# Experts two pair-buckets at a time, members read from the logits' values alone, and the gather's copies issued behind the router's splits

## The chip, the core and the metric

The kernel runs on one core of one Trainium2 chip. The metric is the device time of one execution in microseconds (us). Engines are named as in the profile: PE is the matrix engine (PEld its weight loads), DVE the vector engine, ACT the scalar engine, POOL GpSimd, SP the engine whose queue issues the DMAs.

## What is computed

Two transformer blocks follow each other on 256 tokens of width 1024, all in float32. The first has four SwiGLU feed-forward layers of width 2816, a gated convolution and a differential attention. The second has a sparse attention, a state-space branch, and at its end a mixture of 32 experts, the only part that the change touches:

```
def hier_moe(h, w_rg, b_rg, w_re, b_re, w_gate, w_up, w_down):     # h: [256, 1024], normed
    g_logits = h @ w_rg + b_rg                     # 4 groups
    g_idx = argmax(g_logits); g_w = softmax(g_logits)[g_idx]
    e_logits = (h @ w_re + b_re).reshape(-1, 4, 8) # 8 experts in a group
    e_in = e_logits[g_idx]
    top_v, top_i = top_k(e_in, 2); top_p = softmax(top_v)
    combine = one_hot(g_idx) * (g_w * sum(one_hot(top_i) * top_p))
    for g in range(4):
        act = silu(h @ w_gate[g]) * (h @ w_up[g]) * combine[:, g]
        out = out + act @ w_down[g]                # w_gate, w_up: 8 x [1024, 256]; w_down: 8 x [256, 1024]
```

Each token uses two experts of one group. The weights of all 32 experts, 100.7 MB, are read in any case.

## The kernel before

The tokens lie in two halves of 128 (`i` = 0, 1). Float32 products of weights and activations in the early layers are made of three products of rounded parts (`hi`, `lo`); `split` (L406) makes such a pair with a copy on ACT (L408) and a subtraction on DVE (L409).

**The way into the experts.** `boundary` (L512) ends the layer before (the output projection `wo`, class `OutProj`) and starts the mixture. For each half it adds `wo` to the residual `h` (L1411), takes the mean square on ACT (L430), the root on POOL (L423), the scaled copy `xs` on DVE (L462, `Moe.pre`), transposes it on PE (L470, `Moe.tr`) and splits it into `xTmoh`, `xTmol` (L408, L409). `Moe.chunk` (L1471) then makes the router's logits `rt` with 16 matmuls, one on `xTmoh` and one on `xTmol` in turn (L1478, L1479), and beside them a second split of `xs`, token by row, into `xh[i]` (ACT, L1481) and `xl[i]` (DVE, L1482), which the gather reads later. In what order the instructions stand on an engine is decided by the framework: a list scheduler with a model of the engines takes, on each engine, a ready instruction, first those of higher priority (`hot`), then the earlier in the program. The engines then run their queues in that order. `issue_after` forbids an order.

**The router.** `route` (L1512) works on DVE with small operations. It takes each token's best group, its two best experts with ties broken by the index (`first_max`), the membership `member` of each token in 16 buckets (a bucket is a pair of neighbouring experts), the token's place in its bucket with five small matmuls (L1540 to L1544), and the selection matrix `S[i]` (128 tokens x 16 buckets x 64 slots, L1551). It also works out the weights of the shares (`cwt`).

**The gather.** `gather` (L1587) multiplies `xh`, `xl` with `S` and so brings the tokens of four buckets at a time into `xg` (32 matmuls for four buckets, 4 calls). `shares` (L1601) does the same for the weights.

**The experts.** The loop over 32 experts (`n`) runs `up(n)`, `down_(n-1)`, `turn_(n)`. `up` (L1609) computes gate and up with 16 products (two instructions each) of 64 stationary columns, gate and up in the two halves of the array's columns; ACT takes silu (L1620), DVE multiplies (L1621). `turn_` transposes 64 rows (L1628). `down_` multiplies with `w_down` (L1640). After each second expert the bucket's sum is split (`yg`), `sgt` transposes `S` (four float32 products, L1653), and `scatter` adds the bucket's rows to `h` with eight matmuls over 64 rows (L1665) and four additions on DVE (L1667). The last one also writes the output.

**The weights' ring.** `Ring` (L1415) loads the expert weights in tiles of 512 KB (4 for gate and up, 2 for down of each expert), 192 tiles in all, from SP's queue (L1430). It has 26 places. A place is loaded anew when PE has read the tile in it.

Of the kernel before, what the change touches and what calls it, by code (L numbers as in the profile page):

```python
# [16 lines left out]
P = 128  # L17
T = 256
# [204 lines left out]
def kernel(ctx: ExitStack, tc: tile.TileContext, a: dict, out: bass.AP, upto=99, start=1):  # L223
# [95 lines left out]
    for n in range(33):  # L319
        if n < 32:  # L320
            for w in ("w_gate_2", "w_up_2"):
                v = a[w][0, n // 8, n % 8].rearrange("(p k) c -> p k c", k=KT)
                ring_src += [v[:, k:k + 4] for k in (0, 4)]
        if n > 0:
            d = a["w_down_2"][0, (n - 1) // 8, (n - 1) % 8]
            ring_src += [d[k * P:(k + 1) * P, :] for k in range(2)]
# [1118 lines left out]
    class Moe(Phase):  # L1445
# [4 lines left out]
        def pre(self, i):  # L1450
            if i == 0:
                self.xs = {}
# [4 lines left out]
                self.lg = self.m1.tile([P, 2, 36], F32, name="lg")  # L1457
# [4 lines left out]
                dve.tensor_scalar(self.iotam, cst[:, C_IOTA:C_IOTA + SLOTS], -1000.0, None, op0=ALU.add)  # L1462
                self.xh = [self.m1.tile([P, KT, P], F32R, name=f"xh{i}") for i in range(2)]
# [7 lines left out]
        def chunk(self, i):  # L1471

            x = xT["mo"]
            c = slice(i * P, (i + 1) * P)
            w = W.get(pl["rt"])
            rt = bank("rt")
            for k in range(KT):
                pe.matmul(rt[:, :72], lhsT=x[0][:, k, c], rhs=w[:, k], start=(k == 0), stop=False)  # L1478
                pe.matmul(rt[:, :36], lhsT=x[1][:, k, c], rhs=w[:, k, :36], start=False, stop=(k == KT - 1))  # L1479
            xv = self.xs[i][:, :].rearrange("t (p k) -> t k p", k=KT)  # L1480
            act.activation(self.xh[i], xv, AF.Copy)  # L1481
            dve.tensor_tensor(out=self.xl[i], in0=xv, in1=self.xh[i].bitcast(F32), op=ALU.subtract)  # L1482
            with hot():
                dve.tensor_tensor(out=self.lg[:, i], in0=rt[:, :36], in1=bc[:, B_RT:B_RT + 36], op=ALU.add)
                dve.tensor_tensor(out=self.lg[:, i], in0=rt[:, 36:72], in1=self.lg[:, i], op=ALU.add)
# [26 lines left out]
        def route(self):  # L1512

            tl, b3, first_max = self.tl, self.b3, self.first_max
            tt, red, lg = dve.tensor_tensor, dve.tensor_reduce, self.lg
            el = lg[:, :, 4:36].rearrange("p i (g e) -> p i g e", e=8)
            gl = lg[:, :, 0:4]
# [14 lines left out]
            oo, m4 = tl("oo", 2, 8), tl("m4", 2, 4)  # L1532
            tt(out=oo, in0=o1, in1=o2, op=ALU.add)
            red(m4, oo[:, :, :].rearrange("p i (b s) -> p i b s", s=2), axis=AX, op=ALU.max)
            M = self.m1.tile([P, 2, 16], BF16, name="member")
            for i in range(2):
                tt(out=M[:, i].rearrange("p (g b) -> p g b", b=4), in0=oh[:, i, :, None].to_broadcast([P, 4, 4]),
                   in1=m4[:, i, None, :].to_broadcast([P, 4, 4]), op=ALU.mult)
            rk = bank("rank")
            pe.matmul(rk[:, 0:16], lhsT=self.before, rhs=M[:, 0], start=True, stop=True)  # L1540
            pe.matmul(rk[:, 16:32], lhsT=self.before, rhs=M[:, 1], start=True, stop=False)
            pe.matmul(rk[:, 16:32], lhsT=self.ones, rhs=M[:, 0], start=False, stop=True)
            pe.matmul(rk[:, 32:48], lhsT=self.ones, rhs=M[:, 0], start=True, stop=False)
            pe.matmul(rk[:, 32:48], lhsT=self.ones, rhs=M[:, 1], start=False, stop=True)  # L1544
            self.rank, place = tl("rank", 3, 16), tl("place", 2, 16)
            dve.scalar_tensor_tensor(place, M, -1000.0, rk[:, :32].rearrange("p (i b) -> p i b", b=16), op0=ALU.mult, op1=ALU.add)
            S = self.S = [self.m1.tile([P, 16, SLOTS], F32R, name=f"S{i}") for i in range(2)]

            def put(b0, b1):
                for i in range(2):  # L1550
                    tt(out=S[i][:, b0:b1], in0=self.iotam[:, None, :].to_broadcast([P, b1 - b0, SLOTS]),  # L1551
                       in1=place[:, i, b0:b1, None].to_broadcast([P, b1 - b0, SLOTS]), op=ALU.is_equal)

            put(0, 4)

# [18 lines left out]
            put(4, 16)  # L1574
            dve.tensor_copy(self.rank[:, :, :].rearrange("p i b -> p (i b)"), rk[:, :48])

        def body(self, _):
            m2, tl, tt = self.m2, self.tl, dve.tensor_tensor
            xh, xl = self.xh, self.xl
            with hot():  # L1580
                self.route()
            S = self.S
            xg = [xtp.tile([P, KT, T], F32, name=f"xg{p}0", tag=f"xT{p}") for p in "hl"]
            cwg = tl("cwg", 32)
            acc, hid, hT, yg, sgT = {}, {}, {}, {}, {}

            def gather(q, ks):  # L1587

                for k in ks:
                    b = bank("xg")  # L1590
                    for kk in range(2):
                        for n, (s, i) in enumerate(((xh, 0), (xh, 1), (xl, 0), (xl, 1))):
                            pe.matmul(b[:, kk * T:(kk + 1) * T], lhsT=s[i][:, k + kk], rhs=S[i][:, 4 * q:4 * q + 4].rearrange("p b s -> p (b s)"),
                                      start=(n == 0), stop=(n == 3))
                    d, s = xg[q][:, k:k + 2], b[:, :].rearrange("p (k t) -> p k t", t=T)
                    if k % 4:
                        act.activation(d, s, AF.Copy)
                    else:
                        dve.tensor_copy(d, s)

            def shares(q):  # L1601
                b = bank("cw")
                for j in range(4):
                    for i in range(2):
                        pe.matmul(b[64:, 2 * j:2 * j + 2], lhsT=S[i][:, 4 * q + j].bitcast(F32), rhs=self.cwt[:, i, 8 * q + 2 * j:8 * q + 2 * j + 2],
                                  start=(i == 0), stop=(i == 1))
                dve.tensor_copy(cwg[64:, 8 * q:8 * q + 8], b[64:, :8])

            def up(n):  # L1609
                ring[0] = 0  # L1610
                b = bank("eg")
                ring[0] = 1
                w = [t[:, :].rearrange("p (k c) -> p k c", c=256) for t in ring_w.get(4)]
                x = xg[n // 8][:, :, n // 2 % 4 * SLOTS:(n // 2 % 4 + 1) * SLOTS]
                for k in range(KT):
                    for v in range(2):
                        pe.matmul(b[64 * v:64 * v + 64, :T], lhsT=x[:, k], rhs=w[2 * v + k // 4][:, k % 4], start=(k == 0), stop=(k == KT - 1))  # L1617
                ring_w.done(4)
                s = m2.tile([P, T], F32, name="es", tag="es")
                act.activation(s[64:], b[:64, :T], AF.Silu)  # L1620
                dve.scalar_tensor_tensor(s[64:], s[64:], cwg[64:, n:n + 1], b[64:, :T], op0=ALU.mult, op1=ALU.mult)  # L1621
                hid[n] = s

            def turn_(n):
                b = bank("eT")
                s = hid.pop(n)
                for k in range(2):
                    pe.transpose(b[:, k * SLOTS:(k + 1) * SLOTS], s[64:, k * P:(k + 1) * P], ident[64:, 64:])  # L1628
                t = m2.tile([P, 2, SLOTS], F32, name="hT", tag="hT")
                act.activation(t, b[:, :2 * SLOTS].rearrange("p (k t) -> p k t", t=SLOTS), AF.Copy)  # L1630
                hT[n] = t

            def down_(n):
                p, e = divmod(n, 2)
                if e == 0:
                    acc[p] = accp.tile([P, 512], F32, name=f"ey{p}", tag=f"acc0{p % 2}")
                t = hT.pop(n)
                for k, w in enumerate(ring_w.get(2)):
                    for j in range(2):
                        pe.matmul(acc[p][64 * j:64 * j + 64], lhsT=t[:, k], rhs=w[:, j * 512:(j + 1) * 512],  # L1640
                                  start=(e == 0 and k == 0), stop=(e == 1 and k == 1))
                ring_w.done(2)
                if e == 1:
                    y = two.tile([P, 2, 512], F32R, name="yg", tag="t")
                    split(acc.pop(p), y[:, 0], y[:, 1])
                    yg[p] = y

            def sgt(p):

                b = bank("SgT")  # L1650
                for i in range(2):
                    for j in range(2):
                        pe.matmul(b[64 * j:64 * j + 64, i * P:(i + 1) * P], lhsT=S[i][:, p].bitcast(F32), rhs=ident, start=True, stop=True)  # L1653
                t = m2.tile([P, T], F32R, name="SgT", tag="SgT")
                act.activation(t, b[:, :T], AF.Copy)
                sgT[p] = t

            def scatter(p):
                y, t = yg.pop(p), sgT.pop(p)
                for i in range(2):  # L1660
# [285 lines left out]
```

## Time and profile before

| | |
|---|---|
| median of 3 runs | 1680.09 us (1673.47 to 1680.95) |
| the profiled execution | 1676.58 us, of which the traced span is 1674.8 us |
| PE busy in the span | 1612.4 us (96%) |
| DVE, ACT, POOL busy | 939.2 us (56%), 786.6 us (47%), 139.7 us (8%) |
| read from HBM in the span | 338.22 MB |
| stretch of the experts (first `up` to the last addition) | 1415.7 to 1668.0 us |

Times in the rows are counted from the start of the span. A busy time of PE is no proof that PE is at its peak, since matmuls overlap; where an engine's work stands on the chain that ended last, its own part is read from that chain.

### The profile page before, as it was taken

What the parts mean: (1) busy time and instruction counts of PE and PEld (TensorE: products, weight loads), DVE (VectorE), ACT (ScalarE), POOL (GpSimd) and SP (SyncE); (2) the same over time, 40 slices, a digit from 0 to 9 for tenths busy, and PEclk for the clock granted to TensorE, in tenths of its full rate; (3) what the DMA queues carried; (4) which work ended last, traced back from release to release, by engine and by line L of the source; (5) the groups of instructions that cost most, each with busy time, mean ns of one, the idle gap of its engine ahead of it and who ended that gap; (6) DMA issues with size and microseconds to landing.
All of it is one profiled execution on the core that took longest, in us unless ns stands there. A gap on an engine that the chain in (4) does not pass through costs nothing.

```text
span 1674.8 us, 28506 instructions
## 1 busy us (share of the span) xinstructions
PE 1612.4 (96%) x11550; PEld 1390.4 (83%) x11550; DVE 939.2 (56%) x1429; ACT 786.6 (47%) x1226; POOL 139.7 (8%) x145
## 2 busy tenths in 40 slices
PE   7999999999999999998999999999999997999997
PEld 7999899999989999986899988988989885555543
DVE  5655666755556555476655556977675655232322
ACT  5544454544445444366544445665767633111111
POOL 1000100000010000024200014400221000000000
PEclk9999999999999999999999999999999997999998
DMA  8766474766647666462566645525443854999991
GB/s 286 253 192 188 151 226 127 235 207 188 198 143 226 193 187 199 152 201 76 161 201 193 191 134 152 151 72 176 121 136 103 297 172 190 407 397 388 414 410 57
DMA packets 211656, 341.21 MB, mean 204 GB/s; under 512 B 14612, under 2 KB 166445, under 8 KB 211389
## 3 DMA queue, kind: packets, MB, share of 16 engines
q1 hardware_dynamic: 211485, 339.24, 61.2%
q8 instruction: 93, 1.52, 0.4%
q14 instruction: 46, 0.38, 0.1%
q0 software_dynamic: 32, 0.07, 0.1%
HBM read 338.22 MB, written 1.05 MB: 203 GB/s over the span
## 4 chain that ended last, share of the span: by engine, by line
PE 81%; DVE 8%; ACT 4%; issue 3%; DMA 2%; POOL 1%; SPq 0%; ACTq 0%; POOLq 0%; DVEq 0%
PE eg L1617 7%; PE g L498 4%; PE u L499 4%; PE u L498 4%; PE g L497 4%; PE g L499 4%; PE u L497 4%; PE fo L400 4%; PE fo L398 4%; PE fo L399 4%; PE ey L1640 3%; DVE lo L176 2%; PE sc L1665 2%; PE tk L400 2%; PE tk L399 2%
## 5 line engine op out<-in xcount | busy, mean ns | idle before, releaser
L176 DVE TENSOR_TENSOR lo<-raw,hi 128x1024 fp32r<-128x1024 f32 (+1 forms) x446 | 523.4, 1184 | 372.2 <-ACT hi L171 365.8
L171 ACT ACTIVATE hi<-raw 128x1024 fp32r<-128x1024 f32 (+1 forms) x434 | 456.4, 1058 | 430.4 <-PE g L498 106.4
L497 PE MATMUL u<-xTh_f,hi 128*128 128x256 f32 x608 | 168.3, 277 | 0.0
L498 PE MATMUL g<-xTl_f,hi 128*128 128x256 f32 x608 | 168.1, 276 | 0.2 <-DVE xTl_f L409 0.2
L497 PE MATMUL g<-xTh_f,hi 128*128 128x256 f32 x608 | 168.2, 277 | 0.1
L498 PE MATMUL u<-xTl_f,hi 128*128 128x256 f32 x608 | 168.0, 276 | 0.0
L499 PE MATMUL u<-xTh_f,lo 128*128 128x256 f32 x608 | 168.0, 276 | 0.0
L499 PE MATMUL g<-xTh_f,lo 128*128 128x256 f32 x608 | 167.9, 276 | 0.0
L398 PE MATMUL fo<-hi,hTh 128*128 128x512 f32 x352 | 138.9, 395 | 0.0
L399 PE MATMUL fo<-lo,hTh 128*128 128x512 f32 x352 | 138.2, 393 | 0.0
L400 PE MATMUL fo<-hi,hTl 128*128 128x512 f32 x352 | 137.8, 393 | 0.0
L498 PEld LDWEIGHTS g<-xTl_f,hi 128*128 128x128 f32 x608 | 114.1, 188 | 1.7 <-DVE xTl_f L409 0.4
L497 PEld LDWEIGHTS g<-xTh_f,hi 128*128 128x128 f32 x608 | 114.2, 188 | 1.6 <-DVE xTl_f L409 0.3
L497 PEld LDWEIGHTS u<-xTh_f,hi 128*128 128x128 f32 x608 | 114.2, 188 | 0.1
L499 PEld LDWEIGHTS u<-xTh_f,lo 128*128 128x128 f32 x608 | 114.2, 188 | 0.0
L498 PEld LDWEIGHTS u<-xTl_f,hi 128*128 128x128 f32 x608 | 114.1, 188 | 0.0
L499 PEld LDWEIGHTS g<-xTh_f,lo 128*128 128x128 f32 x608 | 114.1, 188 | 0.0
L423 POOL TENSOR_TENSOR rstd<-var,mhalf 128x1 f32<-128x1 f32 (+1 forms) x41 | 28.0, 683 | 946.4 <-DVE var L421 894.9
L400 PE MATMUL tk<-hi,xTl_at 128*128 128x256 f32 x320 | 90.6, 283 | 0.0
L399 PE MATMUL tk<-lo,xTh_at 128*128 128x256 f32 x320 | 90.5, 283 | 0.0
L398 PE MATMUL tk<-hi,xTh_at 128*128 128x256 f32 x320 | 90.1, 282 | 0.0
L400 PEld LDWEIGHTS fo<-hi,hTl 128*128 128x128 f32 x352 | 66.2, 188 | 15.2
(475 smaller groups left out, 3531.4 us busy)
## 6 DMA issues: line engine op xcount, KB each, us to landing
raw<-in_ffn_w_gu_dram SPq DMA_DIRECT2D x176, 512.0 KB, 4.4
raw<-in_ffn_w_down_dram SPq DMA_DIRECT2D x88, 512.0 KB, 4.3
raw<-in_w_in_dram SPq DMA_DIRECT2D x72, 512.0 KB, 4.0
mw<-in_w_gate_dram SPq DMA_DIRECT2D x64, 512.0 KB, 7.8
mw<-in_w_up_dram SPq DMA_DIRECT2D x64, 512.0 KB, 7.6
mw<-in_w_down_dram SPq DMA_DIRECT2D x64, 512.0 KB, 8.2
raw<-in_conv_w_in_dram SPq DMA_DIRECT2D x24, 512.0 KB, 4.7
raw<-in_w_kv_dram SPq DMA_DIRECT2D x16, 512.0 KB, 5.3
```

The source lines that it names most:

```text
L171: self.order(self.nc.scalar.activation(hi[:q, :n], r[:q, :n], AF.Copy))
L176: self.order(e.tensor_tensor(out=lo[:q, c:c + cut], in0=r[:q, c:c + cut], in1=hi[:q, c:c + cut].bitcast(F32), op=ALU.subtract))
L398: ms = (pe.matmul(ps, lhsT=xh, rhs=wh, start=first, stop=False), pe.matmul(ps, lhsT=xh, rhs=wl, start=False, stop=False), pe.matmul(ps, lh ...
L399: pe.matmul(ps, lhsT=xh, rhs=wl, start=False, stop=False),
L400: pe.matmul(ps, lhsT=xl, rhs=wh, start=False, stop=last))
L423: pool.tensor_tensor(out=r, in0=v, in1=mhalf[:, :n], op=ALU.pow)
L497: pe.matmul(o, lhsT=wh, rhs=x[0][:, k], start=(k == 0), stop=False)
L498: pe.matmul(o, lhsT=wh, rhs=x[1][:, k], start=False, stop=False)
L499: pe.matmul(o, lhsT=wl, rhs=x[0][:, k], start=False, stop=(k == KT - 1))
L1617: pe.matmul(b[64 * v:64 * v + 64, :T], lhsT=x[:, k], rhs=w[2 * v + k // 4][:, k % 4], start=(k == 0), stop=(k == KT - 1))
L1640: pe.matmul(acc[p][64 * j:64 * j + 64], lhsT=t[:, k], rhs=w[:, j * 512:(j + 1) * 512], start=(e == 0 and k == 0), stop=(e == 1 and k == 1))
L1665: pe.matmul(bs[j], lhsT=t[r, i * P:(i + 1) * P], rhs=y[r, q], start=(q == 0), stop=(q == 1))
```

## The change

**Order of the experts.** `steps` pairs expert `e` of bucket 2m with expert `e` of bucket 2m+1: 16 steps of two experts. The ring's order follows. `up` is now a generator that works on one expert of the step at a time and yields between them; the two experts of a step put their result into the upper and the lower 64 rows of one tile.

**Full height.** `turn_` transposes 128 rows at once, `shares` and `sgt` work on two buckets (128 slots) at once, `sgt` with rounded operands (F32R) and an identity `identr`. `scatter` sums over 128 rows, two buckets at a time, and runs half `i` of the tokens after each half of an `up`. `down_` keeps its size, now with four weight tiles at a time and two banks for the sums.

**Members from values.** The logits are put into 2 x 5 rows of 8 (the four groups' logits, filled up with a very low number, are one row). One maximum, one comparison, one second maximum and one comparison over all rows give the members. The weights of the shares are worked out in `weigh`, behind the first gather.

**Copies behind the splits.** `xh[i]` and `xl[0]` must be issued behind what stands on their engine so far, which is the split `xTmoh`, `xTmol` of that half. `xl[1]` is made in four pieces between the pieces of the first gather. The router's matmuls are ordered: first eight on `xTmoh`, then eight on `xTmol`.

```diff
+    steps = [(4 * m + e, 4 * m + 2 + e) for m in range(8) for e in range(2)]
+    for n in range(17):
+        for x in steps[n] if n < 16 else ():
             for w in ("w_gate_2", "w_up_2"):
...
         if n > 0:
+            ring_src += [a["w_down_2"][0, x // 8, x % 8, k * P:(k + 1) * P, :] for x in steps[n - 1] for k in range(2)]
...
             for k in range(KT):
                 pe.matmul(rt[:, :72], lhsT=x[0][:, k, c], rhs=w[:, k], start=(k == 0), stop=False)
+            for k in range(KT):
                 pe.matmul(rt[:, :36], lhsT=x[1][:, k, c], rhs=w[:, k, :36], start=False, stop=(k == KT - 1))
-            act.activation(self.xh[i], xv, AF.Copy)
-            dve.tensor_tensor(out=self.xl[i], in0=xv, in1=self.xh[i].bitcast(F32), op=ALU.subtract)
+            last = {}
+            for x in nc.cur_bb.bb.instructions:
+                last[x.engine] = x
...
+            r = act.activation(self.xh[i], self.xv[i], AF.Copy).ins
+            issue_after(tc, r, last[r.engine])
+            if i == 0:
+                r = dve.tensor_tensor(out=self.xl[i], in0=self.xv[i], in1=self.xh[i].bitcast(F32), op=ALU.subtract).ins
+                issue_after(tc, r, last[r.engine])
             with hot():
+                dve.tensor_tensor(out=self.part[:, i], in0=rt[:, 36:72], in1=bc[:, B_RT:B_RT + 36], op=ALU.add)
+                dve.tensor_tensor(out=self.lg[:, i, 4:40], in0=rt[:, :36], in1=self.part[:, i], op=ALU.add)
...
+            red(top, lg, axis=AX, op=ALU.max)
+            tt(out=eq, in0=lg, in1=top[:, :, None].to_broadcast([P, 10, 8]), op=ALU.is_equal)
+            dve.scalar_tensor_tensor(low, eq, NEG, lg, op0=ALU.mult, op1=ALU.add)
+            red(t2, low, axis=AX, op=ALU.max)
+            tt(out=low, in0=lg, in1=t2[:, :, None].to_broadcast([P, 10, 8]), op=ALU.is_ge)
+            m4 = tl("m4", 2, 5, 4)
+            red(m4[:, :, :, :].rearrange("p i r b -> p (i r b)"), low[:, :, :].rearrange("p r (b s) -> p (r b) s", s=2), axis=AX, op=ALU.max)
+            for i in range(2):
+                tt(out=M[:, i].rearrange("p (g b) -> p g b", b=4), in0=eq[:, 5 * i, 4:8, None].to_broadcast([P, 4, 4]),
+                   in1=m4[:, i, 1:5], op=ALU.mult)
...
             def shares(q):
+                for j in range(2):
                     for i in range(2):
+                        pe.matmul(b[:, 4 * j:4 * j + 4], lhsT=self.S[i][:, 4 * q + 2 * j:4 * q + 2 * j + 2].rearrange("p b s -> p (b s)").bitcast(F32),
+                                  rhs=self.cwt[:, i, 8 * q + 4 * j:8 * q + 4 * j + 4], start=(i == 0), stop=(i == 1))
...
             def turn_(n):
                 for k in range(2):
-                    pe.transpose(b[:, k * SLOTS:(k + 1) * SLOTS], s[64:, k * P:(k + 1) * P], ident[64:, 64:])
+                    pe.transpose(b[:, k * P:(k + 1) * P], s[:, k * P:(k + 1) * P], ident)
...
+                for j in range(2):
+                    for k in range(2):
+                        for x in range(2):
+                            r = slice(64 * x, 64 * x + 64)
+                            pe.matmul(acc[m][j][r], lhsT=t[:, k, r], rhs=w[2 * x + k][:, j * 512:(j + 1) * 512],
+                                      start=(e == 0 and k == 0), stop=(e == 1 and k == 1))
...
             def sgt(m):
                 for i in range(2):
-                    for j in range(2):
-                        pe.matmul(b[64 * j:64 * j + 64, i * P:(i + 1) * P], lhsT=S[i][:, p].bitcast(F32), rhs=ident, start=True, stop=True)
+                    pe.matmul(b[:, i * P:(i + 1) * P], lhsT=self.S[i][:, 2 * m:2 * m + 2].rearrange("p b s -> p (b s)"), rhs=self.identr, start=True, stop=True)
...
+            def scatter(m, i):
+                for j in range(2):
+                    b = accp.tile([P, 512], F32, name=f"sc{j}", tag=f"acc1{j}")
                     for q in range(2):
+                        pe.matmul(b, lhsT=sgT[m][:, i * P:(i + 1) * P], rhs=yg[m, j][:, q], start=(q == 0), stop=(q == 1))
+                    tt(out=halves(h[i])[j], in0=b, in1=halves(h[i])[j], op=ALU.add)
...
             with hot():
+                self.route()
+                for k in range(0, KT, 2):
+                    tt(out=xl[1][:, k:k + 2], in0=self.xv[1][:, k:k + 2], in1=xh[1][:, k:k + 2].bitcast(F32), op=ALU.subtract)
+                    gather(0, k)
+            self.weigh()
+            self.put(4, 16)
...
+            for n in range(16):
+                q = n // 4 + 1
+                for e, _ in enumerate(up(n)):
+                    if n % 2 == 1 and n > 2:
+                        scatter(n // 2 - 1, e)
+                    if q < 4 and n % 4 < 2:
+                        gather(q, 4 * (n % 4) + 2 * e)
                 if n:
                     down_(n - 1)
                 turn_(n)
                 if n % 2:
                     sgt(n // 2)
+                if q < 4 and n % 4 == 2:
+                    shares(q)
```

## Rows read from the trace of the kernel before

**Rows 1.** The page's second part: 40 slices of the span, 41.9 us each.

```profile
PE   7999999999999999998999999999999997999997
...
GB/s 286 253 192 188 151 226 127 235 207 188 198 143 226 193 187 199 152 201 76 161 201 193 191 134 152 151 72 176 121 136 103 297 172 190 407 397 388 414 410 57
```

**Rows 2.** Windows: stretch, length, busy time by engine, PE's clock, DMA share, GB/s.

```profile
1410.00:1412.00 2.00, 2.00 (x11) 2.00 (x11) 1.58 (x5) 0.00 (x0) 0.00 (x0) 0.50 0.00 0
1440.00:1460.00 20.00, 20.00 (x144) 10.54 (x141) 5.80 (x10) 2.89 (x7) 0.00 (x0) 1.00 1.02 408
1540.00:1560.00 20.00, 20.00 (x143) 12.11 (x144) 6.71 (x11) 3.44 (x9) 0.00 (x0) 1.00 1.03 418
1640.00:1660.00 20.00, 19.15 (x126) 9.01 (x124) 6.21 (x10) 2.62 (x7) 0.00 (x0) 1.00 0.00 1
```

**Rows 3.** The DMA view of 1410 to 1675 us: 40 slices, and the transfers' queue.

```profile
GB/s 0 228 409 417 406 418 404 392 329 374 416 421 416 411 420 366 363 387 360 420 420 417 417 412 416 421 412 375 402 413 422 418 419 406 48 0 0 0 115 57
...
q1 hardware_dynamic: 24480, 88.09, 83.9%
```

**Rows 4.** The chain that ended last, 1415.5 to 1675 us, shares by engine and line.

```profile
by line: PE eg L1617 47.2%; PE ey L1640 21.0%; PE sc L1665 11.1%; PE xg L1593 5.3%; PE SgT L1653 3.6%; PE eT L1628 3.1%; PE cw L1605 1.1%; DVE yg L409 1.1%; DVE es L1621 1.0%; ACT yg L408 0.9%; DVE h L1667 0.8%; ACT es L1620 0.7%; issue 0.4
```

**Rows 5.** Pieces of that chain: start, length (us), engine, tile, line, instructions.

```profile
1415.68 6.96 PE eg L1617 x63
...
1477.67 2.31 PE eg L1617 x20
...
1486.27 0.67 PE sc L1665 x4
...
1490.96 0.27 PE eT L1628 x2
1491.22 0.59 PE SgT L1653 x8
```

**Rows 6.** Timeline: start, length, engine, line, operation, shapes, count, idle time before.

```profile
1379.20 0.39 PE L399 MATMUL wo<-lo,xTh_mg 128*128 128x512 f32 x1
...
1379.43 0.39 PE L400 MATMUL wo<-hi,xTl_mg 128*128 128x512 f32 x1
...
1383.78 1.04 PE L470 MATMUL xT<-cst,xs 128*128 128x128 f32 x8
...
1417.29 0.33 SPq L1430 DMA_DIRECT2D mw<-in_w_down_dram  x1
...
1526.33 1.92 PEld L1617 LDWEIGHTS eg<-mw,xgl 128*64 128x64 f32 x20 [0.36 <-issue]
...
1644.95 0.20 PEld L1628 LDWEIGHTS eT<-cst,es 64*128 64x128 f32 x2 [1.05 <-DVE es L1621]
```

**Rows 7.** The chain into the experts, 1386 to 1415 us, pieces as above.

```profile
1386.40 2.00 DVE xl L1482
...
1393.27 0.67 DVE xs L462
...
1393.97 2.07 ACT xh L1481
...
1396.06 2.00 DVE xl L1482
...
1398.72 0.40 PE rt L1479
...
1402.14 0.21 DVE lg L1484
...
1406.91 0.15 DVE member L1537
...
1408.35 6.31 PE xg L1593 x32
```

**Rows 8.** The chain's last pieces.

```profile
1660.96 1.80 PE ey L1640 x8
...
1667.28 0.69 DVE h L1667
```

More of the change, by code (lines that the diff above doesn't have):

```diff
@@ L1531, in route @@
             o2 = first_max(e8b, 8, t2, "o2")
[L1532 to L1554, printed above, removed]
             dg = tl("dg", 2, 4)
@@ L1579, in body @@
             xh, xl = self.xh, self.xl
-            with hot():
-                self.route()
-            S = self.S
             xg = [xtp.tile([P, KT, T], F32, name=f"xg{p}0", tag=f"xT{p}") for p in "hl"]
             cwg = tl("cwg", 32)
[L1585 to L1599, printed above, removed]
+            hid, hT, acc, yg, sgT = {}, {}, {}, {}, {}
@@ new lines, in gather @@
+            def gather(q, k):
+                b = bank("xg")
+                for kk in range(2):
+                    for n, (s, i) in enumerate(((xh, 0), (xh, 1), (xl, 0), (xl, 1))):
+                        pe.matmul(b[:, kk * T:(kk + 1) * T], lhsT=s[i][:, k + kk], rhs=self.S[i][:, 4 * q:4 * q + 4].rearrange("p b s -> p (b s)"),
+                                  start=(n == 0), stop=(n == 3))
+                d, s = xg[q][:, k:k + 2], b[:, :].rearrange("p (k t) -> p k t", t=T)
+                if k % 4:
+                    act.activation(d, s, AF.Copy)
+                else:
+                    dve.tensor_copy(d, s)
@@ L1609, in up @@
+                dve.tensor_copy(cwg[:, 8 * q:8 * q + 8], b[:, :8])
             def up(n):
[L1610 to L1622, printed above, removed]
+                s = hid[n] = m2.tile([P, T], F32, name="es", tag="es")
+                for e, x_ in enumerate(steps[n]):
+                    ring[0] = 0
+                    b = bank("eg")
+                    ring[0] = 1
+                    w = [t[:, :].rearrange("p (k c) -> p k c", c=256) for t in ring_w.get(4)]
+                    x = xg[x_ // 8][:, :, x_ // 2 % 4 * SLOTS:(x_ // 2 % 4 + 1) * SLOTS]
+                    gate, own = slice(64 - 64 * e, 128 - 64 * e), slice(64 * e, 64 * e + 64)
+                    for k in range(KT):
+                        for v, r in enumerate((gate, own)):
+                            pe.matmul(b[r, :T], lhsT=x[:, k], rhs=w[2 * v + k // 4][:, k % 4], start=(k == 0), stop=(k == KT - 1))
+                    ring_w.done(4)
+                    act.activation(s[own], b[gate, :T], AF.Silu)
+                    dve.scalar_tensor_tensor(s[own], s[own], cwg[own, x_:x_ + 1], b[own, :T], op0=ALU.mult, op1=ALU.mult)
+                    yield
@@ L1642, in down_ @@
[L1642 to L1648, printed above, removed]
+                w = ring_w.get(4)
+                for j in range(2):
[4 more added lines that the diff above has]
+                                      start=(e == 0 and k == 0), stop=(e == 1 and k == 1))
+                    if e == 1:
+                        y = two.tile([P, 2, 512], F32R, name="yg", tag="t")
+                        split(acc[m][j], y[:, 0], y[:, 1])
+                        yg[m, j] = y
@@ L1655, in sgt @@
                 act.activation(t, b[:, :T], AF.Copy)
[L1656 to L1660, printed above, removed]
-                    bs = [accp.tile([P, 512], F32, name=f"sc{j}", tag=f"acc1{j}") for j in range(2)]
-                    for q in range(2):
-                        for j in range(2):
-                            r = slice(64 * j, 64 * j + 64)
-                            pe.matmul(bs[j], lhsT=t[r, i * P:(i + 1) * P], rhs=y[r, q], start=(q == 0), stop=(q == 1))
-                    for j in range(2):
-                        tt(out=halves(h[i])[j], in0=bs[j], in1=halves(h[i])[j], op=ALU.add)
-                        if p == 15:
-                            nc.sync.dma_start(out[0, i * P:(i + 1) * P, j * 512:(j + 1) * 512], halves(h[i])[j])
```

88 lines of the change are left out of this document (48 added, 40 removed).

## The prediction

> **What bounds the kernel now.** I read the page's slices first: DMA moves around 200 GB/s for most of the span, but about 400 in the slices from the 35th to the 39th [rows 1], and these are the experts. There two resources could be the bound, so I took the windows next. From 1440 to 1560 us PE is busy without a break, and DMA's share is 1.02 to 1.03 at 408 to 418 GB/s: both are full. From 1640 to 1660 us DMA moves nothing while PE still works 19.15 of 20 us [rows 2]. The 40 slices of the DMA view say the same: the last weights land in slice 35, about 1637 us, and PE goes on for 30 us [rows 3]. So the weights are always ahead, PE sets the end, and DMA is close behind as the next limit. The chain of waits confirms it: from 1415.5 us on it is PE's for more than nine tenths (eg, ey, sc, xg, SgT, eT, cw) [rows 4]. Ahead of the first `up` stands a second piece, from the residual to the gather, in which small steps of ACT, DVE and PE wait for each other and PE runs at the lower of its two clock levels (granted 0.50) [rows 7, 2].
>
> I call the start of the first `up` T0 = 1415.7 [rows 5]. The last `down_` ends at 1660.96 + 1.80 = 1662.8 [rows 8], so T0 + 247.1. What follows (split, scatter, additions, output) I leave as it is. The sum therefore needs the shift of T0 and the new length from T0 to the last `down_`.
>
> **The way into the experts.** (a) *Half 0's copies.* `xl[0]` holds DVE from 1386.40 to 1388.40, right ahead of the residual's addition for half 1 on the chain [rows 7]. Behind the splits, the addition can go about 2 us earlier. But the scheduler is greedy, and `xh[0]` and `xl[0]` may still get in before the mean square; bounds 0 and 3.2 (the 2.0 and what `xh[0]` holds up), I take 2.0. Their cost is hidden by PE's router matmuls of half 0. If that cover is gone, they cost 4.
>
> (b) *Half 1's copies.* `xh[1]` (2.07) and `xl[1]` (2.00) stand on the chain between `xs` (ends 1393.94) and the router (1398.72) [rows 7]: 4.8 us, of which the rest is only transposes and splits that partly ran beside them. Without them the way is transposes of half a tile (0.5 of 1.04 [rows 6], doubled at the low clock), one ACT piece and one DVE piece of half a tile (about 0.6 each): 2.2 to 2.3. Gain 2.5; bounds 0 and 4.1.
>
> (c) *Order of the router's matmuls.* Now the second matmul of each pair waits for `xTmol`, and the chain runs 3.4 us from 1398.72 to 1402.14. With the eight of `xTmoh` first, half of these go beside the split on DVE: gain 1.7, bounds 0 and 1.7.
>
> (d) *Members from values.* From 1402.14 to the end of `member` (1407.06) some 25 small DVE operations take 4.9 us, 0.2 each [rows 7]. The new list has one addition behind the last matmul (`part` can go earlier), seven wide operations on 80 elements and two for `M`. At 0.2 to 0.25 each this is 2.1: gain 2.8. `weigh` still has the rest, some 25 operations, 5 us. It lies beside the gather (6.31 us on PE [rows 7]) and the first `up` and is needed only by DVE's first product with the shares. Cost nothing; were the cover gone, 3 us.
>
> (e) *`xl[1]` in four pieces* now stands on DVE ahead of the gather: 2.0 in all, one piece of 0.5 ahead of the first matmul, the others beside a gather that needs one every 1.6 us. Cost 0.5, bounds 0 and 2.
>
> Sum: 2.0 + 2.5 + 1.7 + 2.8 - 0.5 = 8.5 us for T0, bounds 3 (a scheduler that lets the copies in again) and 11.
>
> **The experts on PE.** The chain's shares times 259.3 us give eg 122.4, ey 54.5, sc 28.8, xg 13.7, SgT 9.3, eT 8.0, cw 2.9, and 12.7 of waits for other engines and issue [rows 4].
>
> *eg.* 63 instructions in a row take 6.96, 20 take 2.31 [rows 5]: 0.108 each and 0.15 for each piece. 1024 of them are 110.6, so the 122.4 hold about 79 pieces. The trace shows what a piece costs: after a matmul of another shape (64 rows, or the full array) PEld stands idle for 0.36 with no one to wait for [rows 6]. The change leaves the matmuls and takes away interruptions: one turn instead of two, one scatter half per half step, one `sgt` in four experts. I count 48 pieces (32 at least, 79 at most). Gain 4.7, bounds 0 and 7.
>
> *sc.* 16 buckets cost 28.8, 1.8 each, though four matmuls in a row take 0.67 [rows 4, 5]. The new form is 64 matmuls of 128 rows by 512. Full-height matmuls of this size start 0.23 apart [rows 6]: 14.7, and 16 pieces of 0.15: 17.0. Gain 11.8. The Trainium skill ("TensorEngine Tiling (Array Packing)", Theoretical Speedup) speaks against this step: a contraction of 64 rows already runs up to twice as fast as two tiles side by side, so by that page of the Trainium skill full height would save no array time and this term would be 0. The trace's own numbers meet it halfway: four 64-row matmuls in 0.67 are 0.17 each, 128 of them 21.4, so the array gains 6.7 and the rest of the 11.8 is interruption. Bounds 0 and 14.
>
> *SgT.* 128 instructions, 9.3. New: 16 with 128 columns. Eight of 128x128 take 1.04, 0.13 each [rows 6]: 2.1. Gain 7.2. No row shows this operation with rounded operands; at twice the price it is 5.1.
>
> *eT.* 64 instructions, 8.0. New: 32 of 0.13 and 16 pieces of 0.1: 5.8. Gain 2.2. *cw.* Half as many, each twice as wide: gain 1.0, bounds 0 and 1.5. *xg, ey.* Same matmuls, same shapes: 0.
>
> *Waits.* In the last steps each expert makes PE wait 1.05 for `es` [rows 6], since nothing is left to put between. Two experts now share one turn, and the scatter between the halves has a whole half `up` to free its bank: I take 5 of the 12.7, bounds 0 and 10. What is new is that the sums of `down_` use both banks for each pair of buckets where they alternated; the next `down_` comes a step later, and the two splits take 2.6 us, so nobody waits.
>
> Sum: 4.7 + 11.8 + 7.2 + 2.2 + 1.0 + 5 = 31.9. By PE alone the last `down_` ends at T0 + 215.2.
>
> **The experts on DMA.** From the first reload, 1417.29 [rows 6], or T0 + 1.6, 88.09 MB move to the end, 1.05 of them output [rows 3]: 87.0 MB of weights. At the 418 GB/s of the best window [rows 2] this is 208, plus 1 for the start, and then three quarters or more of the last `down_`, twice 1.80 [rows 8]: 3. Earliest end T0 + 213.8. So the two limits nearly meet; each delay of the one while the other lags is not won back, for which I add 2 to PE's: T0 + 217. Gain 247.1 - 217 = 30.1.
>
> **Sum.** 1676.6 (the profiled execution) - 8.5 - 30.1 = 1638.0. The profiled execution lies 3.5 below the median of three runs, which spread over 7.5; I add half of it: **1640**.
>
> **The rivals.**
> *DMA takes over early.* From 1417.3 to 1637 us the 87.0 MB moved at only 396 GB/s on average, with slices down to 329 and 360 [rows 3]. If these dips are the memory's and not a PE that freed its places late, the weights take 219.7 again, the end is T0 + 225 and the gain 22. Then the time is 1648. For it: four slices in a row, from 1509 to 1536 us, stand at 360 to 387. Against: most stand at 410 to 421.
>
> *The copies come back into the chain.* The change forbids one order only. If the scheduler puts `xh`, `xl` and the pieces where somebody waits, T0 moves by 3: 1646. With the rival above: 1653.
>
> *Full height is worth nothing.* Two 64-row matmuls side by side may be as quick as a full one, with the same interruptions; then the 11.8 of sc are missing: 1652. This is what the table of the Trainium skill named above would give. Against: sc's 28.8 on the chain are a third more than the 21.4 its matmuls need in a row.
>
> *Slower than before: PE starves and its clock falls.* If PE waits for tiles in every step, it can drop to the lower level, as ahead of the gather, where it is granted 0.50 while busy [rows 2]. A step of 13 us would then take some 24, so the 38 gained are gone after 3.5 steps; from 4 of 16 on the kernel is slower, with 6 steps 1676 - 38 + 66 = 1704. Against: with gaps of 1.05 in each of the last experts the clock stayed at 1.00 [rows 2, 6], and a slow PE lets the ring fill again.
>
> **Chances.** Forecast (1632 to 1645) 0.58; DMA early 0.16; copies in the chain 0.12; both 0.03; full height worth nothing 0.05; slower 0.03; something unseen within half a per cent of before 0.03. The range 1630 to 1654 leaves out the last ones and the low end of the first. A measurement can tell about 0.5% (8 us) from no change, and all cases but the last two lie beyond it: faster 0.93, same 0.03, slower 0.04.
>
> **What would show each step.** T0 near 1407, with `xTmoh` right behind the transposes, no `xh`, `xl` between `xs` and the router, and some ten DVE operations from the router to `member`. On the chain from T0: eg 115 to 118, sc 17, SgT 2, eT below 6, ey and xg unchanged. The stretch from the last landing to the last `down_` shrinks from 26 us to a few; if it shrinks to 3, DMA has become the bound, and PE then shows waits for `mw`. A T0 that stays, or an sc that stays above 25, would make the forecast wrong, and most of all a granted clock below 1.00 between 1420 and 1620 us.

## The result, and the profile after

The changed kernel takes 1651.53 us (median of 4 runs, 1649.27 to 1655.16) where the kernel before takes 1678.57 beside it: ratio 0.9845, 95% interval 0.9815 to 0.9875, so 27 us less. The forecast was 1640, 38.6 less. The time lies inside the range, but 11.5 of the 38.6 us are missing, and they are the question of what follows. The profiled execution spans 1647.5 us.

First the way into the experts. These are pieces of the chain that ended last: start, length, engine, tile, line, and how many instructions.

```profile
1391.48 1.98 PE xT L470 x8
...
1393.48 0.60 ACT xTmoh L408
1394.08 2.02 ACT xh L1490
...
1396.12 2.17 DVE xl L1694 x4
1398.29 0.11 DVE part L1496
...
1398.43 0.21 DVE lg L1497
...
1400.50 0.17 DVE member L1539 x2
...
1401.88 6.08 PE xg L1612 x32
1407.96 4.47 PE eg L1640 x38
```

T0 is 1407.96 where it was 1415.68 [rows 5, 7]: 7.7 us earlier, 8.5 were forecast. `xTmoh` stands right behind the transposes, and the members come 2.0 us behind `lg` instead of 4.7. The four pieces of `xl[1]` slipped ahead of `part`, which they hold up by 1.3: the router's last matmul ends at 1396.87, and `part` starts at 1398.21.

Then the experts. The chain from T0 on, shares by engine and line, and the moved data over 40 slices from 1410 to 1648 us (GB/s):

```profile
by line: PE eg L1640 50.2%; PE ey L1665 27.6%; PE sc L1686 7.8%; PE xg L1612 5.4%; PE eT L1650 2.5%; PE cw L1624 1.4%; DVE h L1687 0.9%; PE SgT L1677 0.7%; ACT yg L408 0.5%; DVE es L1643 0.2%; issue 0.2%; ACT es L1642 0.2%
```
```profile
GB/s 286 328 348 408 419 419 420 412 414 421 419 419 417 411 417 420 419 416 414 416 417 420 420 419 410 419 420 415 419 414 416 415 419 419 414 354 13 3 91 96
```

The shares times the 239.5 us of this window stand beside those of [rows 4]:

| on the chain from T0, us | before | forecast | after |
|---|---|---|---|
| eg | 122.4 | 117.7 | 120.2 |
| ey | 54.5 | 54.5 | **66.1** |
| sc | 28.8 | 17.0 | 18.7 |
| SgT | 9.3 | 2.1 | 1.7 |
| eT | 8.0 | 5.8 | 6.0 |
| xg, cw | 16.6 | 15.6 | 16.3 |
| waits | 12.7 | 7.7 | 4.8 |

Most rows come near their forecast (`eg` lies 2.5 above it). One does not: `ey`, entered at nothing, costs 11.6 us more. The granted clock was 1.00 from the first `up` to the last `down_`, and tiles were not late: from 1434 us on the DMA works at 410 to 421 GB/s, without the dips of [rows 3], and of the last 40 tiles each whose landing the trace holds lands 8.9 us or more ahead of its use. The last lands at 1624.5 and the last `down_` ends at 1637.5, 13 us later (26 before).

What happened to `ey` shows in the timeline of TensorE (start, length, engine, line, operation, operands, count):

```profile
1530.77 0.40 PE L1612 MATMUL xg<-S,xl 128*128 128x256 f32 x2
1531.10 1.93 PE L1665 MATMUL ey<-mw,hT 128*64 128x512 f32 x4
1532.95 0.51 PE L1612 MATMUL xg<-S,xh 128*128 128x256 f32 x2
```

A matmul of `down_` fills 64 of the 128 columns of the array and stands twice in the trace (two passes). Here four passes take 1.85 us, 0.46 each; eight in a row took 1.80 before [rows 8], 0.225 each. The order in which the instructions stand says why. Somewhat later in the changed kernel:

```
L1665 MATMUL ey0<-mw124,hT   64x512
L1665 MATMUL ey1<-mw124,hT   64x512
L1665 MATMUL ey0<-mw126,hT   64x512
L1665 MATMUL ey1<-mw126,hT   64x512
...
L1665 MATMUL ey0<-mw125,hT   64x512
L1665 MATMUL ey1<-mw125,hT   64x512
L1650 MATMUL eT<-cst,es   128x128 x2
...
L1665 MATMUL ey0<-mw127,hT   64x512
L1665 MATMUL ey1<-mw127,hT   64x512
```

On the chain this stretch is (the first piece is mw124 with mw126, the last mw127 alone):

```profile
1554.85 1.77 PE ey L1665 x8
...
1558.35 1.23 PE ey L1665 x3
1559.58 0.37 PE eT L1650 x2
...
1560.74 1.86 PE ey L1665 x4
```

mw124 and mw125 belong to the expert in one column half, mw126 and mw127 to the other: `eT`, on the whole array, stands between the second tiles of the two. Before, the two column halves of `down_` read the *same* tile, so both were ready at once and stood side by side. Now each half has tiles of its own, which arrive one after the other. The four are also loaded in the order in which they are used here, 124, 126, 125, 127: the scheduler goes by arrival, and a half goes alone, with operations on the whole array ahead of it or behind.

### The profile page after: what moved, and what is told of

Read it like the earlier page. It is cut to its first block, busy times and chain, and to the rows that moved or that the text cites. A ratio compares the mean times of both kernels' runs of the same rounds, so it can differ in the third digit from the quotient of the medians.

```text
span 1647.5 us, 27933 instructions
## 1 busy us (share of the span) xinstructions
PE 1593.7 (97%) x11310; PEld 1387.5 (84%) x11310; DVE 917.4 (56%) x1406; ACT 779.8 (47%) x1202; POOL 139.7 (8%) x145
## 4 chain that ended last, share of the span: by engine, by line
PE 81%; DVE 7%; ACT 4%; issue 3%; DMA 2%; POOL 2%; SPq 0%; ACTq 0%; POOLq 0%; DVEq 0%
PE eg L1640 7%; PE g L498 4%; PE g L497 4%; PE u L499 4%; PE g L499 4%; PE u L498 4%; PE u L497 4%; PE fo L398 4%; PE fo L400 4%; PE fo L399 4%; PE ey L1665 4%; DVE lo L176 2%; PE tk L400 2%; PE tk L399 2%; PE tk L398 2%
## 5 line engine op out<-in xcount | busy, mean ns | idle before, releaser
L1643 DVE SCALAR_TENSOR_TENSOR es<-es,cwg,eg 64x256 f32<-64x256 f32 x32 | 15.3, 478 | 116.1 <-ACT es L1642 116.0
```

The source lines that it names most:

```text
L1643: dve.scalar_tensor_tensor(s[own], s[own], cwg[own, x_:x_ + 1], b[own, :T], op0=ALU.mult, op1=ALU.mult)
```

## The experiments

Each kernel is compared with runs of the kernel before on the same chip. The part ahead of the experts is the same code in all, yet the first output-projection matmul (`wo`, 1362.47 in the changed kernel) starts between 1360.9 and 1370.6 us in the fourteen profiled executions, one of each kernel. So beside the medians I give the *stage*: the span of the profiled execution less the start of `wo`. It rests on one execution each. Its first part repeats well: T0 comes 45.1 to 45.7 us behind the start of `wo` in all kernels with the changed way in up to e10, and 53.0 to 53.2 in the two without it (before, e2). e8 and e9 ran twice, the others four to ten times.

| kernel | median, us | ratio to before, 95% | stage, us |
|---|---|---|---|
| before | 1678 to 1680 | 1 | 312.5 |
| changed | 1651.5 | 0.9815 to 0.9875 | 285.0 |
| e1 way in only | 1674.9 | 0.9967 to 0.9986 | 305.5 |
| e2 experts only | 1659.8 | 0.9866 to 0.9901 | 292.9 |
| e3 `down_` paired | 1651.4 | 0.9820 to 0.9853 | 283.0 |
| e4 `up` paired too | 1645.3 | 0.9790 to 0.9823 | 278.5 |
| e5 e3, turn behind | 1649.1 | 0.9802 to 0.9835 | 278.2 |
| e6 e4 in ring order | 1646.5 | 0.9770 to 0.9830 | 279.2 |
| e7 scatter of 64 rows | 1683.6 | 1.0018 to 1.0037 | 315.2 |
| e8 runs of two | 1651.7 | 0.9812 to 0.9851 | 284.0 |
| e9 halves apart | 1702.5 | 1.0116 to 1.0156 | 335.1 |
| e10 runs of four | 1673.9 | 0.9940 to 0.9969 | 305.6 |
| e11 e4, four more tiles | 1643.0 | 0.9750 to 0.9798 | 275.3 |
| e12 all together | 1642.6 | 0.9766 to 0.9800 | 274.1 |

**The two parts alone** (e1, e2): the lines of the way in, or those of the experts, put into the other kernel.

> The way into the experts as changed, the experts themselves and the order of their tiles as before. Theory: the two parts add up, and this one is worth the 7.7 us by which the first `up` came earlier in the changed kernel (1415.68 to 1407.96): about 1671 us, the first `up` near 1408, and 247 us from there to the end of the last `down_`, as before. Rival: the stream of expert tiles sets the end, and an earlier start of TensorE only makes it wait for tiles: then the last `down_` ends where it did, 1662.8, and the time stays at 1678.

> The way into the experts as before, the experts as changed (two pair-buckets at once, full-height scatter and transposes). Theory: the experts alone are worth 17.6 us by the traces (247.1 to 229.5 from the first `up` to the end of the last `down_`) and about 2 behind it: 1659 us, with `ey` on the chain near 66 us as in the changed kernel (54.5 before). Rival: the experts lost 11 us on `ey` only because TensorE came earlier to tiles that were not there; starting 7.7 us later it has them, `ey` falls to 55 to 58 and the time is 1652, the same as with both parts.

The experts alone give 19.0 us by the medians and 19.6 by the stage, as expected, with `ey` at 27.4% of 240 us, 66 again. So a TensorE that arrives 8 us later finds its tiles no better, and that rival falls. The way in alone gives 7.0 in the stage and 4.0 (2.4 to 5.5) in the medians; 7.7 were expected. By the stage the parts add up, 26.6 to 27.5; by the medians 4 us are lacking. In the trace the whole gain of the way in is there (T0 is 45.7 us behind the start of `wo`), so what lacks lies elsewhere. I have no cause for it: it stays open.

**Pairs kept** (e3: `down_`, the tile that lands last first, all in one chain; e4: `up` in the same way).

```
-                    for k in range(2):
-                        for x in range(2):
+                    for k in (1, 0):
+                        for x in (1, 0):
...
+                            issue_after(tc, o, prev)
```

> The changed kernel with the matmuls of `down_` kept in pairs that fill both column halves of the array: the one that needs the tile landing last comes first, and each is issued behind the one before it. No work is added or left out. Theory: `ey` grew from 54.5 to 66.1 us on the chain because the order by tile arrival broke the pairs, and a matmul alone takes 0.43 us with half of the array idle where a pair takes the same: `ey` goes back to 55 to 58 us. The tiles cannot land earlier, and those of the last `up` lie 5 us ahead of their use, so of the 9 to 11 us some 5 to 8 reach the end: 1644 to 1647 us. Rival: `ey` is slower because its two halves now read two different tiles, or because the transfers fill the memory: then the order changes nothing, `ey` stays near 66 and the time at 1651 to 1652.

> As the last, and the gate and up matmuls of `up` kept in pairs as well, the tile that lands last first. Theory: fewer broken pairs of `eg`, at most 1 to 3 us on the chain (120.2 now), but every `up` now starts only when its fourth tile is there: 1642 to 1647 us, the slack between landing and use falls to nothing in the last steps, and waits for tiles show on the chain. Rival: starting each `up` at its last tile costs what a tile takes to come, 1.25 us, times three in each step that has no slack, 5 to 15 us in all: 1650 to 1660.

In e3 `ey` falls to 59.2 us on the chain (57.5 without the low clock told at the end; 54.5 before), so most of its growth came from the broken pairs. But hardly any of it reaches the end, and the 1644 to 1647 expected did not come. Its chain and its waits say where it went:

```profile
by line: PE eg L1640 50.7%; PE ey L1666 24.9%; PE sc L1690 8.5%; PE xg L1612 5.4%; PE eT L1650 2.7%; PE cw L1624 1.4%; DVE es L1643 1.3%; DVE h L1691 1.0%; ACT es L1642 1.0%; PE SgT L1681 0.7%; issue 0.4%
```
```profile
PE eT L1650 <- DVE es L1643: 5.7, 6, 1.0
```

The lone `ey` matmuls had stood between the last `eg` and the transposes `eT`, and had covered the wait for `es`. Now that wait is open, 5.5 us of chain (2.3% of 237.6) for 1.0. Another 1.7 went to the clock. So the 11.6 on `ey` were never all loss: part of it filled waits, which fits with the waits in the table, 2.9 under the forecast.

With `up` paired too (e4) 6.2 us are gained on the changed kernel by the medians, 6.5 in the stage, and the bound changes. The chain near the end:

```profile
1594.76 10.06 DMA mw<-in_w_up_dram
...
1604.88 9.92 DMA mw<-in_w_gate_dram
...
1614.86 10.17 DMA mw<-in_w_down_dram
...
1625.08 6.23 PE ey L1670 x28
```

Thirty us of transfers stand on it, and in the last three steps the last tile of each group lands 0.0 to 1.8 us ahead of its use (8.9 or more in the changed kernel). The last lands 217.2 us behind T0.

**Is it the tiles?** (e5, e6, e11)

```
e5, on e3:  turn_: + if n: issue_after(tc, o, ylast)     # behind down_(n - 1)
e6, on e4:  pairs with k ascending, turn_ as in e5
e11, on e4: + once = [m2.tile([P, 2 * UNIT], F32, name=f"once{p}", tag=f"xg{p}", bufs=1) for p in "hl"]
            + ring_w.add(None, [o[:, v * UNIT:(v + 1) * UNIT] for o in once for v in range(2)])
```

> As the run that kept the matmuls of `down_` in pairs, and the transposes of each step issued behind the `down_` of the step before. In that run `ey` on the chain fell from 66.1 to 59.2 us, but the transposes came straight behind the last `eg` of their step and TensorE waited for `es` (ACT and DVE es 5.5 us of the chain, 1.0 in the changed kernel). Theory: the lone `ey` matmuls of the changed kernel had filled that wait; with the pairs as a block ahead of the transposes the wait is covered and `ey` stays under 60: 3 to 6 us less than the 1651.4 of that run, so 1645 to 1648, and no wait of `eT` for `es` but in the first steps. Rival: the tiles set the pace behind TensorE's back (they land 4 to 8 us ahead of use in the last steps), and the wait only moves to them: 1650 to 1652.

> Pairs kept in `up` and `down_`, transposes behind `down_`, and the pairs taken in the order in which the ring's tiles were loaded, so that the tile that the next load needs first is also free first. In the run with both pinned (last tile first) the time was 1645.3, 30 us of the chain were tiles under way, and from 10 to 30 us behind the first loads the memory moved only 243 and 371 GB/s against 306 and 354 in the changed kernel and 404 to 420 later. Theory: the stream of tiles is the bound now, and it starts as soon as the first tiles are given back; in ring order it fills 1 to 4 us sooner: 1641 to 1645 us, last landing within 217 us of the first `up`. Rival: TensorE is still the bound and saves nothing by the ring's order: 1645 to 1648.

> The run with all pairs kept (1645.3), and the ring of tiles longer by four for the first round: the room of `xTmo` (the router's operands, free from the router's end until the third gather needs it) takes four tiles once. Nothing else changes. Theory: with the pairs kept the stream of tiles is the floor (in that run no tile of the last three steps landed more than 1.8 us ahead of its use), and it stood still from 1398 to 1411 us because the ring was full; four tiles of 1.25 us less to load later give 3 to 5 us: 1640 to 1642 us, and slack of 2 us or more in the last steps. Rival: TensorE and the way behind the last tile set the end: no change, 1644 to 1647.

e5 closes the waits for `es` and wins 4.8 us on e3 in the stage (1.7 of it e3's low clock); by the medians 2.3, with intervals that overlap, and 1649.1 lies between its two sides. By the stage it ends where e4 does, by another way, with transfers on its chain (12.8% for `w_down_2` alone); by the medians it lies 3.8 above e4, with intervals that overlap too. e6 ends there as well: its stream starts no faster (244 and 356 GB/s in its first two stretches of 10 us, 243 and 371 in e4), and its last tile lands 217.0 us behind T0, so ring order is worth nothing. Three different orders with one stage, 278.2 to 279.2, speak for a floor outside TensorE: the last tile lands 216.6 to 217.2 us behind T0 in all three, and 216.5 already in the changed kernel. e11 moves that floor: its last tile lands 213.6 us behind T0, no transfer is left on its chain, and the stage is 3.2 shorter, as forecast for four tiles; the medians (2.3) cannot tell that from nothing by themselves.

**What does a broken pair cost?** (e8, e9, e10: `down_` in one chain, orders of its eight matmuls)

```
e8:   for j: x1 x1, x0 x0          # runs of two
e10:  x1 x1 x1 x1, x0 x0 x0 x0     # runs of four
e9:   x1 x1 x1 x1, eT eT, x0 x0 x0 x0
```

> The run with `down_` in pairs, with one thing turned round: the four matmuls of one column half first, then the four of the other, so that all but the middle pair of each `down_` are broken. Theory: a matmul of 512 columns by itself takes 0.43 us in each of its two passes where a pair takes the same together, so each `down_` goes from 3.6 to 6.5 to 6.9 us, 16 times: 46 to 53 us more than 1651.4, some of it covering waits: 1692 to 1705 us, `ey` near 105 us on the chain. Rival: broken pairs are no cost, since something else made `ey` longer: 1651 to 1656.

> The run with `down_` in pairs, turned round more than the last time: the four matmuls of one column half, then the transposes of the next step (they use the whole array), then the four of the other half. The last run showed runs of two matmuls in one half at no cost: the other half's, queued behind them, ran beside them. Theory, as it now stands: what costs is work of one half that has no work of the other half between two operations on the whole array. Here that is eight passes of 0.43 us on each side of the transposes, 6.9 us a step where a pair takes 3.4: 50 us more in 15 steps, less some 3 to 6 us of waits for `es` that are now covered: 1651 + 44 to 50 = 1695 to 1701 us. Rival: the order of the matmuls costs nothing anywhere, as the last run says on its face: 1648 to 1653.

> As the one before, without the transposes between: four matmuls of one half, then at once the four of the other. Theory (work of both halves between two whole-array operations is laid side by side whatever its order): as with runs of two, 1650 to 1656 us. Rival (it looks ahead only a little, enough for runs of two matmuls with their four passes, not for four with eight): up to 3.4 us in each of 16 steps, 1680 to 1705.

e8 cost nothing, and with it fell my theory in its first form, that order alone decides. Its eight matmuls take what pairs take:

```profile
1534.50 3.71 PE L1666 MATMUL ey<-mw,hT 128*64 128x512 f32 x16
```

In e9, where the transposes separate the halves, each half needs that time for itself, and the run takes 51 us more than e3, a little over the 44 to 50 expected:

```profile
1511.39 0.44 PE L1650 MATMUL eT<-cst,es 128*128 128x128 f32 x2
1511.75 3.65 PE L1668 MATMUL ey<-mw,hT 128*64 128x512 f32 x8
1515.33 0.44 PE L1687 MATMUL SgT<-identr,S 128*128 128x128 f32 x2
```

e10 lies between, 22 us above e3, and neither side had that. Two windows of one `down_`, its matmuls alone (length, busy time of PE with its passes, PEld, DVE, ACT, then clock, DMA share, GB/s):

```profile
1497.30:1499.09 1.79, 1.76 (x4) 0.60 (x5) 0.00 (x0) 0.00 (x0) 1.00 1.04 417
```
```profile
1499.09:1501.00 1.91, 1.91 (x10) 0.85 (x9) 0.00 (x0) 0.00 (x0) 1.00 1.03 418
```

Four passes start one by one in the first 1.8 us, and the other half starts beside the fifth of eight. In e8, with runs of four passes, both halves start at once. So in these runs the halves run side by side however their work is ordered, as long as no more than four passes of one half are ahead; an operation on the whole array waits for both. Counting each kernel's order of instructions by that (0.43 us a pass of 512 columns, half of it for 256) gives an estimate of eg and ey together:

| eg + ey, us | counted | on the chain |
|---|---|---|
| before | 170.8 | 176.9 |
| changed | 179.8 | 186.3 |
| e3 | 170.0 | 178.0 (without 1.7 of low clock) |
| e7 | 186.7 | 196.4 |
| e9 | 225.3 | 235.3 |
| e10 | 194.8 | 200.0 |

The count lies 5 to 10 below throughout, and its differences agree: changed less before 9.0 against 9.4 measured. With every half paired it would be 164.8.

**Full height** (e7).

```
+                for x in range(2):     # row half x for j = 0, the other for j = 1
+                    r = slice(64 * (x ^ j), 64 * (x ^ j) + 64)
+                    pe.matmul(bs[j], lhsT=sgT[m][r, ...], rhs=yg[m, j][r, q], ...)
```

> The changed kernel with the scatter alone back on 64-row operands: 128 scatter matmuls and 64 additions as before the change, in place of 64 and 32; transposes, `SgT` and the experts as changed. Theory: a matmul of 64 rows takes as long as one of 128 (28.8 us of the chain before, 18.7 now, at half the number), so the scatter is again near 29 us on the chain and the time 1651.5 + 8 to 11 = 1660 to 1662. Rival: 64-row matmuls in alternate halves of the array run side by side, two in the time of one, and full height is worth nothing: 1651 to 1653.

It cost 32 us, far more than either side expected. The scatter is at 12.7% of 268 us, 34.0, and eg and ey are 10 dearer (196.4 against 186.3), 7 of them by the count of broken pairs above. Two rows from its timeline:

```profile
1484.17 0.74 PE L1688 MATMUL sc<-yg,SgT 64*128 64x512 f32 x4
...
1490.55 0.73 PE L1688 MATMUL sc<-yg,SgT 64*128 64x512 f32 x2
```

Four 64-row matmuls of both row halves take as long as two of one. The Trainium skill ("TensorEngine Tiling (Array Packing)", Theoretical Speedup) gives 64-row work up to twice the speed; the first row agrees with that and the second shows when it fails, namely when the other half has nothing to do. The full-height form has no halves to break. But since this run broke pairs that the kernel before kept, it doesn't give the price of full height alone: for that the chain's 28.8 to 18.7 stands.

**All together** (e12): e11 with the turn of e5, `xl[1]` behind `member` and `S`, `weigh` behind `S`.

> As the last run (pairs kept, four tiles more in the first round), with the transposes behind `down_`, and three edits ahead of the experts: the pieces of `xl[1]` behind `member` and `S` and not ahead of `part`, and the sums of `weigh` behind `S` and not between the steps to the members. In the last run the first gather matmul came 1.0 us later behind the output projection than in the changed kernel (39.4 us after its start there, 40.4 here), since `weigh` had slipped between; `xl[1]` held `part` up by 1.0 to 1.2. Theory: the tiles are the floor again by the last steps (they land 0.9 to 1.6 us ahead of use), their stream starts again with the first `up`, and that comes 2 us earlier: 1643.0 - 2 = 1640 to 1642 us. Rival: the open waits of `eT` for `es` (1.7 us, and 6.7 at the weight loads) are what TensorE still loses, and closing them gives 3 to 5 us: 1637 to 1640. Other rival: none of this reaches the end, 1643 to 1645.

The first gather matmul comes 38.0 us behind the start of `wo` (39.4 in the changed kernel), but T0 only 0.4 sooner, since the gather now waits for the pieces of `xl[1]` and lasts 7.1 us for 6.1. DVE needs those 2.2 us somewhere. In e11 too the gather began at 39.4, not at 40.4 as the expectation has it; it was T0 that came 0.9 later there. Against e11 T0 is 1.3 sooner and the stage 1.2 shorter, and the medians show nothing of it (1642.6 against 1643.0). The chain holds some 90 us of transfers, so the tiles are the floor again, as the theory had it, though its 1640 to 1642 were just missed:

```profile
by line: PE eg L1643 28.5%; DMA mw<-in_w_up_dram 21.4%; PE ey L1674 15.1%; DMA mw<-in_w_down_dram 12.9%; PE xg L1614 6.9%; DMA mw<-in_w_gate_dram 4.2%; PE sc L1698 4.0%; PE eT L1656 1.4%; PE cw L1626 1.1%; DVE h L1699 1.1%; issue 0.4%; PE S
```

The run is clearly below both kernels: its ratio's interval, 0.9766 to 0.9800, ends under that of the changed kernel.

## Why the prediction was right, and what it missed

The direction, the bound and the range held; of 38.6 us 27 came. That the time lies in the range is in part luck: 1651.5 misses the forecast's own 1632 to 1645 and lies among the times of the rivals, and none of the rivals accounts for it.

- *Way into the experts*, 8.5 forecast, 7.7 in the trace. `lg` of half 1 ends 3.7 earlier (1398.64 against 1402.35 [rows 7]), where (a), (b), (c) and (e) had 5.7 together; `xl[1]` in pieces cost 1.3 ahead of `part` and not 0.5 ahead of the gather, and `xl[0]` (1387.79 to 1389.79) still stands ahead of the mean square's next step. (d) gave 2.7 of 2.8. A further 1.3, not forecast, came from `member` to the first `up`.
- *eg* 2.2 of 4.7. The term was mis-sized: the chain has 68 pieces and not 48 (78 before), as lone `ey` and `sc` matmuls cut into `up`. Nor are pieces all of it: in e3 they are 52, and `eg` is still 120.4.
- *sc* 10.1 of 11.8, *SgT* 7.6 of 7.2, *eT* 2.0 of 2.2; *cw* and *xg* 0.3 of 1.0. Right in kind and size. The rival that full height is worth nothing falls.
- *ey: "Same matmuls, same shapes: 0."* This is the step that failed. The matmuls and shapes are the same, but no longer which tile each half reads, and so not when each is ready. It measured +11.6 on the chain. Keeping the pairs of `down_` alone takes `ey` to 59.2 and gives next to nothing at the end (e3); keeping those of `up` too gives 6.2 to 6.5 (e4). The rest had covered waits or meets the tiles' floor.
- *Waits* 7.9 of 5, better than forecast, which that same cover explains.
- *DMA*: "earliest end T0 + 213.8" was too early. In e4 the last tile lands at T0 + 217.2 and the last `down_` ends at T0 + 222.2, 5.0 behind it where 3 were put. The stream needs some 20 us to reach its full rate (243 and 371 GB/s in the first two stretches of 10 us, e4), while its queue waits 21.2 us in all for `eg` to give back places. In the changed kernel itself the floor did not bind. The reason that the rival "DMA takes over early" gave falls, since the dips are gone (410 to 421 GB/s); transfers set the end only once the pairs were mended.
- *PE starves and its clock falls*: not in the changed kernel.

The sum of the misses: eg and ey 14.1 us over forecast, sc, eT, xg and cw 2.6, way in 0.8; against that waits 2.9, SgT 0.4, the 1.8 added for two limits that meet, and some 2 less behind the last `down_` (10.0 us to the end of the span, 12.1 before). That leaves 10.4 of the 11.5. With pairs kept and four tiles more, 37 us of gain are there (e11).

## What to carry to other kernels

When two matmuls share the array as halves, "same matmuls, same shapes" costs nothing only if the work of both halves still stands close together, with no operation on the whole array between: look at which tiles each half reads before and after, since here a scheduler that goes by arrival parted them. Work that a wait had covered is not free to remove, so ask of each saved matmul what stood beside it. When two resources are both near full, mend the one and look for the other's floor at once, here by giving it a longer buffer.

## Not expected of the hardware

A half of the array took up its work while up to four passes of the other half, standing earlier in the order, were not yet done, and no more (e8, e10).

Between the first `up` and the last `down_` the clock fell once in the fourteen traces, in e3. TensorE had been busy without a break since 1549.91, then stood still for 1.03 us ahead of `eT`, did two transposes and eight matmuls of 4 columns, and was then granted 0.60 and 0.55 while busy. Windows: length, busy times, then granted clock, DMA share, GB/s.

```profile
1561.00:1563.00 2.00, 0.97 (x11) 0.91 (x9) 0.49 (x1) 0.75 (x2) 0.00 (x0) 1.00 1.02 410
1563.00:1565.00 2.00, 2.00 (x9) 0.77 (x11) 0.17 (x1) 0.01 (x1) 0.00 (x0) 0.60 1.03 420
1565.00:1567.00 2.00, 2.00 (x8) 0.64 (x6) 0.00 (x0) 0.09 (x1) 0.00 (x0) 0.55 1.03 422
1567.00:1569.00 2.00, 2.00 (x11) 0.61 (x7) 0.69 (x1) 0.83 (x2) 0.00 (x0) 1.00 1.02 418
```

Its passes there start 0.84 us apart for 0.43, the lower of the two levels (1.2 GHz). The `down_` took 5.28 us for 3.58, so 1.7. At 1549.91 a gap of 0.99 ahead of the same transposes, with `SgT` and `ey` behind them, did not do it. What tells the two apart was not tried.
